# Latent attention in a two-layer decoder: keys' high and low parts in one moving operand, second-block values as whole float32, and a finer step list

## The chip, the cores and the metric

The kernel runs on one core of a Trainium2 chip. TensorE (PE) does matmuls and transposes into PSUM banks of 128 x 512 float32; VectorE (DVE), ScalarE (ACT) and GpSimd (POOL) work on SBUF and PSUM; SyncE (SP) issues the loads of weights. Each engine takes its instructions in order and waits on semaphores for the others. The metric is the device time of one execution in microseconds (us); lower is better.

## The reference

Two layers over 256 tokens of width 1024. Layer 0 mixes tokens by "forgetting" attention, layer 1 by latent attention (MLA) with 16 heads; each layer has two half-step feed-forward blocks, a layer norm after every part, and a gated input embedding. Only the latent attention is touched here:

```
c_q = rms_norm(x @ w_dq, q_norm)
q = einsum('bsc,chd->bshd', c_q, w_uq)            # 128 plain + 64 rotary columns a head
scores = (q_nope . k_nope + rope(q_rope) . k_rope) * 192**-0.5
w = softmax(where(key <= query, scores, -inf))    # two blocks of 128 queries
o = w @ v                                         # 16 heads of 128 columns
mix = o.reshape(256, 2048) @ w_o
```

The keys, the rotary key and the values come from one compressed tensor of 256 columns. All of it is float32.

## The kernel before, in words

**Float32 by parts.** A matmul of float32 values is done as three matmuls on `fp32r` operands: every operand is kept as a high part (a rounding copy, made by ScalarE) and a low part (value less high part, made by VectorE), and the product is high x high + high x low + low x high. `mm3` issues the three; `parts` makes both parts of a tile. Transposes use plain float32.

**Weights.** `Stream` loads weight blocks in the order of use into three `raw` buffers and splits each into slots (`hl`, and tiles lent by others: `ota`, `otb`, `qk`, `fs`). A split is one ScalarE copy and one VectorE subtraction, 512 to 1024 columns wide. When a split is made depends on a running estimate of each engine's time (`S.busy`) in `pump`, or on steps in the list: `f n` splits until n units are ready, `a` starts a split's copy when its load should have landed, `l` issues the subtraction left open by `a`.

**The step list.** The latent attention (`mla`) is a list of steps, `ORDER`, played one by one; each step issues instructions to one or more engines, and the list alone sets in which order each engine meets them. The steps of head h:
- `gen h`: 15 matmuls into one bank of ring `h` give the head's keys (right half) and queries (left half), then parts into `qk[h % 2]`.
- `QK h`: scores into a bank of ring `tr`. Query block 0 needs keys 0 to 127 (columns 0 to 127 of the bank), block 1 all 256 keys (columns 128 to 383). Each block gets the three products of `mm3` and two for the rotary part (`zT` with the high and the low part of `kr`).
- `sm h`: VectorE adds the mask and takes the row's minimum of the negated score (two instructions, L1470), ScalarE exponentiates and sums (L1475).
- `div h how`: a reciprocal and two scalings, on VectorE (0) or ScalarE (1).
- `T h`: three transposes of 128 columns (block 0; block 1 with keys 0 to 127; block 1 with keys 128 to 255), then parts into `PT`, of which there is one buffer.
- `AV h`: values times weights into a bank of ring `h`: three 256-wide matmuls with the values of keys 0 to 127, three 128-wide ones with those of keys 128 to 255; then parts into `otb` or `ota`.
- `O h t`: the head's share of the output product, six 512-wide matmuls for one half of the tokens.

`V g t` makes the values of four heads for keys 128t to 128t+127, `vlo` their low part. `rope`, `rot`, `zT`, `zs`, `zU` and `rc` prepare rotary queries. Rings `h` and `tr` have two banks each, `y` four.

Of the kernel before, what the change touches and what calls it, by code (L numbers as in the profile page):

```python
# [46 lines left out]
ORDER = (  # L47
# [26 lines left out]
)  # L74


# [14 lines left out]
class Recorder:  # L91
# [7 lines left out]
    def pump(self, *a, **k):  # L99
        pass  # L100

    lend = reclaim = check = load = busy = pair = split = split_pieces = ahead = later = split_now = fill = pump
    between, hl, hold = {}, {}, False


class Stream:
# [173 lines left out]
    def pair(self, n):  # L280

        self.busy(act=n)
        self.dve_t = max(self.dve_t, self.act_t + 100)
        self.busy(dve=n)

# [112 lines left out]
class Trunk:  # L398
# [97 lines left out]

    def parts(self, hi, lo, src):

        self.nc.scalar.activation(hi, src, AF.Copy)  # L499
        self.nc.vector.tensor_tensor(lo, src, hi.bitcast(F32), op=ALU.subtract)  # L500
        self.S.pair(cols(src))

    def transposed(self, t, src, halves=(0, 1), ring="tr"):

# [767 lines left out]
    def mla(self, li):  # L1272
# [34 lines left out]
        def V(g, t):  # L1307
            w = self.use(("kvv", g))
            ps = vps[g, t] = self.bank(("h", "y", "tr")[VRING[g][t]])
            for k in range(2):  # L1310
                self.mm3(
                    ps, lambda i: self.ckv[:, i, 256 * k + 128 * t : 256 * k + 128 * t + 128],
                    lambda i: w[:, i, 512 * k : 512 * k + 512], k == 0, k == 1,
                )
            o = v[t, g] = self.tl([128, 2, 512], F32R, "g4", 5)
            nc.scalar.activation(o[:, 0, :], ps, AF.Copy)
            S.busy(act=512)

        def vlo(g, t):
# [107 lines left out]
        st, PT = {}, {}  # L1427

        def gen(h):
            if h == 0:  # L1430
                home["qk"] = self.own([128, 2, 2, 512], F32R, "qk")
            ps = self.bank("h")
            hp, s = h // 2, h % 2
            w = self.use(("kvk", hp))
            for k in range(2):
                self.mm3(
                    ps[:, 256:512], lambda i: w[:, i, 256 * k + 128 * s : 256 * k + 128 * s + 128],
                    lambda i: self.ckv[:, i, 256 * k : 256 * k + 256], k == 0, k == 1,
                )
# [7 lines left out]
            self.parts(o[:, 0, :], o[:, 1, :], ps)  # L1447
# [15 lines left out]
        def softmax(h):  # L1463
# [3 lines left out]
            P = self.tl([128, 768], F32, "P", 2)[:, 0:384]  # L1467
            seg = ((0, 128), (128, 384))
            for q, (c0, c1) in enumerate(seg):
                nc.vector.tensor_tensor_reduce(  # L1470
                    out=b[:, c0:c1], in0=b[:, c0:c1], in1=self.mask[:, c0:c1],
                    op0=ALU.add, op1=ALU.min, scale=-scale, scalar=3.0e38, accum_out=nm[:, q : q + 1],
                )
            for q, (c0, c1) in enumerate(seg):
                nc.scalar.activation(  # L1475
                    P[:, c0:c1], b[:, c0:c1], AF.Exp, bias=nm[:, q : q + 1], scale=-1.0,
                    accum_out=su[:, q : q + 1],
                )
            self.S.busy(act=900, dve=600)
            st[h] = P, su  # L1480

        def divide(h, how):
            P, su = st[h]
            nc.vector.reciprocal(su[:, 0:2], su[:, 0:2])
            for q, (c0, c1) in enumerate(((0, 128), (128, 384))):
                if how == 0:
                    nc.vector.tensor_scalar(P[:, c0:c1], P[:, c0:c1], su[:, q : q + 1], None, op0=ALU.mult)
# [8 lines left out]
        def T(h):  # L1496
# [6 lines left out]
            PT[h] = o  # L1503

        OT = []

# [5 lines left out]
        def AV(h):  # L1512
            if h in (0, 10):
                OT.append(self.own([128, 4, 2, 256], F32R, "ota" if h else "otb"))
            o = PT.pop(h)
# [11 lines left out]
            self.parts(ot[:, 0, :], ot[:, 1, :], ps[:, 0:256])  # L1527

        y = [[None] * 2 for _ in range(2)]

# [15 lines left out]
        def hold(x):  # L1546
# [1 line left out]

        steps = dict(
            dq=dq, rms=rms, dqs=dq_scale, cqT=cq_transpose, V=V, vlo=vlo, qr=q_rope, rope=rope, rc=rope_copy, rot=rotate, zT=zT_first,  # L1550
            zs=z_split, zU=zT_last, gen=gen, QK=QK, sm=softmax, div=divide, T=T, AV=AV, O=O, y=room, hold=hold,
            f=S.fill, a=S.ahead, l=S.later, XT=lambda t, n: self.XT(t, (n,)),
            exp=lambda: self.ready_for(AF.Exp), gb=lambda: self.load_gb(li, 1),
            lend=lambda: S.lend("qk"), ln=lambda t: self.ln(t, y[t], ALPHA, LN_EPS),
# [119 lines left out]
```

## Time and profile before

| | |
|---|---|
| time, median of 3 runs (range) | 1069.97 us (1069.09 to 1071.38) |
| the profiled execution: time, span | 1069.07 us, 1067.3 us |
| mean granted TensorE clock | 0.998 |
| PE records | 7236 |
| latent attention, some 705 to 835 us of the span | 130 us |

The time of a run includes some 1.8 us around the span. In rows of groups the numbers after the bar are busy time in us and the mean of one instruction in ns, then the idle time of the engine just before them. PE matmuls are pipelined, so what one costs is read from the start of one to the start of the next. A plain float32 matmul appears as two records, one on `fp32r` or a transpose as one.

### The profile page before, as it was taken

What the parts mean: (1) busy time and instruction counts of PE and PEld (TensorE: products, weight loads), DVE (VectorE), ACT (ScalarE), POOL (GpSimd) and SP (SyncE); (2) the same over time, 40 slices, a digit from 0 to 9 for tenths busy, and PEclk for the clock granted to TensorE, in tenths of its full rate; (3) what the DMA queues carried; (4) which work ended last, traced back from release to release, by engine and by line L of the source; (5) the groups of instructions that cost most, each with busy time, mean ns of one, the idle gap of its engine ahead of it and who ended that gap; (6) DMA issues with size and microseconds to landing.
All of it is one profiled execution on the core that took longest, in us unless ns stands there. A gap on an engine that the chain in (4) does not pass through costs nothing.

```text
span 1067.3 us, 17503 instructions
## 1 busy us (share of the span) xinstructions
PE 1056.7 (99%) x7236; PEld 970.6 (91%) x7236; DVE 718.1 (67%) x1029; ACT 542.6 (51%) x805; POOL 68.1 (6%) x94
## 2 busy tenths in 40 slices
PE   9999999999999999999999999999999999999996
PEld 8989998999889999998899998989999889898986
DVE  6675555878797545458966464578887886454566
ACT  5564442667645434444565454436675466354431
POOL 0000000233200000000330000000000000000000
PEclk9999999999999999999999999999999999999999
DMA  8885643543348655454487555413434568555502
GB/s 299 325 295 215 247 162 119 186 175 121 115 180 301 232 186 192 146 203 139 169 294 259 180 194 187 154 59 123 137 140 158 198 244 308 181 204 182 191 4 79
DMA packets 33091, 199.58 MB, mean 187 GB/s; under 512 B 3698, under 2 KB 5490, under 8 KB 12148
## 3 DMA queue, kind: packets, MB, share of 16 engines
q1 hardware_dynamic: 33012, 198.47, 51.8%
q8 instruction: 57, 0.93, 0.4%
q14 instruction: 22, 0.18, 0.1%
HBM read 197.40 MB, written 1.05 MB: 186 GB/s over the span
## 4 chain that ended last, share of the span: by engine, by line
PE 97%; issue 1%; POOL 0%; DVE 0%; ACT 0%; DMA 0%; SPq 0%; DVEq 0%; ACTq 0%; POOLq 0%
PE y L490 36%; PE h L490 35%; PE tr L490 23%; PE tr L494 2%; DMA raw<-in_w_dram 0%; PE h L494 0%; PE tr L1087 0%; DVE x L575 0%; POOL fs L957 0%; POOL fs L950 0%; ACT hl L194 0%; SPq L360 0%; SPq L476 0%; POOL fs L956 0%; ACT hl L232 0%
## 5 line engine op out<-in xcount | busy, mean ns | idle before, releaser
L195 DVE TENSOR_TENSOR hl<-raw,hl 128x1024 fp32r<-128x1024 f32 (+2 forms) x260 | 305.7, 1194 | 146.7 <-ACT hl L194 146.1
L194 ACT ACTIVATE hl<-raw 128x1024 fp32r<-128x1024 f32 (+2 forms) x260 | 262.9, 1031 | 183.4 <-PE y L490 97.5
L490 PE MATMUL h<-xT,hl 128*128 128x256 f32 x1584 | 187.8, 278 | 1.1 <-DVE hl L234 0.5
L490 PEld LDWEIGHTS h<-xT,hl 128*128 128x128 f32 x1584 | 184.3, 189 | 2.5 <-ACT xT L499 0.9
L490 PE MATMUL y<-hl,g 128*128 128x512 f32 x792 | 185.6, 390 | 0.0
L490 PEld LDWEIGHTS y<-hl,g 128*128 128x128 f32 x792 | 147.5, 188 | 29.8
L490 PE MATMUL tr<-xT,hl 128*128 128x256 f32 x1464 | 170.8, 277 | 0.0
L490 PEld LDWEIGHTS tr<-xT,hl 128*128 128x128 f32 x1464 | 168.6, 188 | 0.5
L490 PE MATMUL h<-hl,xT 128*128 128x512 f32 (+2 forms) x294 | 65.2, 373 | 0.0
L490 PEld LDWEIGHTS h<-hl,xT 128*128 128x128 f32 x294 | 51.9, 188 | 9.7 <-DVE xT L500 0.3
L490 PE MATMUL y<-hl,xT 128*128 128x512 f32 (+3 forms) x330 | 59.7, 331 | 0.0
L490 PEld LDWEIGHTS y<-hl,xT 128*128 128x128 f32 x330 | 50.1, 188 | 5.6 <-ACT xT L499 0.4
L567 POOL TENSOR_TENSOR rs<-ve,mhalf 128x1 f32<-128x1 f32 x16 | 15.1, 943 | 619.3 <-DVE ve L566 619.3
L500 DVE TENSOR_TENSOR g<-P,g 128x512 fp32r<-128x512 f32 x38 | 26.3, 693 | 26.6 <-ACT g L499 26.6
L490 PE MATMUL y<-hl,otb 128*128 128x512 f32 x168 | 42.9, 396 | 0.0
L499 ACT ACTIVATE xT<-tr 128x512 fp32r<-128x512 f32 x28 | 16.2, 597 | 48.8 <-PE tr L494 48.8
L499 ACT ACTIVATE g<-P 128x512 fp32r<-128x512 f32 x38 | 24.0, 632 | 32.7 <-DVE P L684 32.7
L195 DVE TENSOR_TENSOR qk<-raw,qk 128x1024 fp32r<-128x1024 f32 (+2 forms) x23 | 28.0, 1217 | 16.1 <-ACT qk L194 16.1
L195 DVE TENSOR_TENSOR otb<-raw,otb 128x1024 fp32r<-128x1024 f32 (+1 forms) x22 | 26.5, 1206 | 17.7 <-ACT otb L194 17.7
L490 PEld LDWEIGHTS y<-hl,otb 128*128 128x128 f32 x168 | 30.2, 188 | 5.6
L194 ACT ACTIVATE otb<-raw 128x1024 fp32r<-128x1024 f32 (+1 forms) x22 | 22.9, 1039 | 19.4 <-PE y L490 10.8
L194 ACT ACTIVATE qk<-raw 128x1024 fp32r<-128x1024 f32 (+2 forms) x23 | 24.0, 1045 | 16.3 <-PE tr L490 6.6
(264 smaller groups left out, 1431.9 us busy)
## 6 DMA issues: line engine op xcount, KB each, us to landing
raw<-in_ffn_in_dram SPq DMA_DIRECT2D x85, 1024.0 KB, 5.0
raw<-in_ffn_out_dram SPq DMA_DIRECT2D x44, 1024.0 KB, 5.0
raw<-in_pg_dram SPq DMA_DIRECT2D x8, 1024.0 KB, 4.8
raw<-in_mo_dram SPq DMA_DIRECT2D x8, 1024.0 KB, 4.7
raw<-in_kq_dram SPq DMA_DIRECT2D x8, 640.0 KB, 4.1
gb<-in_ln_g_dram SPq DMA_DIRECT2D x8, 512.0 KB, 5.8
gb<-in_ln_b_dram SPq DMA_DIRECT2D x8, 512.0 KB, 7.7
raw<-in_fk_dram SPq DMA_DIRECT2D x4, 1024.0 KB, 4.8
```

The source lines that it names most:

```text
L194: nc.scalar.activation(hi, src, AF.Copy)
L195: nc.vector.tensor_tensor(lo, src, hi.bitcast(F32), op=ALU.subtract)
L490: self.nc.tensor.matmul(out, lhsT, rhs, start=start, stop=stop)
L494: self.nc.tensor.transpose(out, in_, self.ident)
L499: self.nc.scalar.activation(hi, src, AF.Copy)
L500: self.nc.vector.tensor_tensor(lo, src, hi.bitcast(F32), op=ALU.subtract)
L567: nc.gpsimd.tensor_tensor(rs, ve, self.mhalf, op=ALU.pow)
```

## The change

**Scores.** For query block 0 the high query part meets the key's high and low part side by side, as one 256-wide moving operand (`o[:, :, 256:384]`), and the rotary queries meet the high and low rotary keys likewise (`kr[:, 0 : r + 1 : r, 0:128]`). The bank then holds two partial sums for block 0, in columns 0 to 127 and 128 to 255; the low query part (128 wide) goes to the first. Block 1 moves to columns 256 to 511 and keeps its five matmuls.

**Softmax.** `sm` is divided into `mi` and `ex`. `mi` has a new first instruction: VectorE adds the mask to the second partial sum and writes it to SBUF; that tile takes the mask's place in the first masking instruction. The reciprocal is a step of its own, `rec`. Five divisions (heads 2, 3, 4, 10 and 12) go to ScalarE.

**Values.** Those of keys 128 to 255 (`V g 1`) stay whole float32, with no low part and no `vlo`. The third transposed block is copied whole by ScalarE (`tr`, into the tile `negc`, one buffer), and parts are made of the other two only. `AV` ends in one plain float32 matmul of 128 columns.

**Steps.** The making of parts is taken out of `gen`, `T` and `AV` into steps: `ga`, `ta`, `oa` for the high and `gd`, `td`, `od` for the low parts. The list is a new one.

```diff
-            for q0, c0, c1 in ((0, 0, 128), (128, 128, 384)):
-                w = c1 - c0
-                self.mm3(
-                    b[:, c0:c1], lambda i: o[:, i, q0 : q0 + 128],
-                    lambda i: o[:, i, 256 : 256 + w], True, False,
-                )
-                for i in (0, 1 + (h % 2 if h < 8 else 1)):
-                    self.mm(b[:, c0:c1], zT[:, h, q0 : q0 + 128], kr[:, i, 0:w], False, i > 0)
+            r = 1 + (h % 2 if h < 8 else 1)
+            two = b[:, 0:256].rearrange("p (i c) -> p i c", i=2)
+            self.mm(two, o[:, 0, 0:128], o[:, :, 256:384], True, False)
+            self.mm(b[:, 0:128], o[:, 1, 0:128], o[:, 0, 256:384], False, False)
+            self.mm(two, zT[:, h, 0:128], kr[:, 0 : r + 1 : r, 0:128], False, True)
+            self.mm3(
+                b[:, 256:512], lambda i: o[:, i, 128:256], lambda i: o[:, i, 256:512], True, False)
+            for i in (0, r):
+                self.mm(b[:, 256:512], zT[:, h, 128:256], kr[:, i, :], False, i > 0)
...
+            t = P[:, 384:512]
+            nc.vector.tensor_tensor(t, b[:, 128:256], self.mask[:, 0:128], op=ALU.add)
+            seg = ((0, b[:, 0:128], t), (128, b[:, 256:512], self.mask[:, 128:384]))
...
-            self.parts(o[:, 0, :], o[:, 1, :], b[:, 0:384])
+            raw = self.tl([128, 384], F32, "negc", 1)[:, 0:128]
+            left["T", h] = o[:, 0, 0:256], o[:, 1, 0:256], b[:, 0:256]
+            left["raw", h] = raw, b[:, 256:384]
...
-            for m, (i, jj) in enumerate(((0, 0), (0, 1), (1, 0))):
-                self.mm(
-                    ps[:, 128:256], v[1, g][:, i, c : c + 128], o[:, jj, 256:384], False, m == 2
-                )
+            self.mm(ps[:, 128:256], v[1, g][:, c : c + 128], raw, False, True)
+            S.busy(pe=128)
...
-    "f 3", "div 1 0", "rc 0", "f 2", "vlo 1 1", "V 2 0", "f 2", "gen 2", "T 0", "f 2", "gen 3", "f 1", "AV 0",
+    "f 2", "gen 3", "f 2", "tr 0", "ga 3", "AV 0", "rc 1", "y", "oa 0", "T 1", "gd 3", "l", "ta 1", "td 1", "a",
```

Where instructions stand. First TensorE, from the transposes of head 1 (`tr<-ident,P`) over the scores of head 2 (`tr<-qk`, `tr<-fs,xT`) to the value product of head 1 (`h<-PT,g4`), before:

```order
L494 MATMUL tr_7395<-ident_68,P_7311 128x128 x3
L490 MATMUL tr_7408<-qk_7221 128x128 x3
L490 MATMUL tr_7408<-fs_6382,xT_72 128x128 x2
L490 MATMUL tr_7408<-qk_7221 128x256 x3
L490 MATMUL tr_7408<-fs_6382,xT_72 128x256 x2
L490 MATMUL y_7421<-hl3_7267,otb_7381 128x512 x3
L490 MATMUL y_7422<-hl3_7267,otb_7381 128x512 x3
L490 MATMUL h_7441<-PT_7399,g4_7071 128x256 x3
L490 MATMUL h_7441<-PT_7399,g4_7046 128x128 x3
```

and now, where `negc` is the raw block:

```order
L510 MATMUL tr_7391<-ident_68,P_7307 128x128 x3
L506 MATMUL tr_7412<-qk_7220 128x256
L506 MATMUL tr_7412<-qk_7220 128x128
L506 MATMUL tr_7412<-fs_6382,xT_72 128x256
L506 MATMUL tr_7412<-qk_7220 128x256 x3
L506 MATMUL tr_7412<-fs_6382,xT_72 128x256 x2
L506 MATMUL h_7429<-PT_7395,g4_7071 128x256 x3
L506 MATMUL h_7429<-negc_7396,g4_7046 128x128
L506 MATMUL y_7388<-hl3_7276,otb_7379 128x512 x3
L506 MATMUL y_7389<-hl3_7276,otb_7379 128x512 x3
```

Ten score matmuls have become eight and six value matmuls four, and head 0's output product now stands behind head 1's value product.

ScalarE at the same place, from the keys of head 3 (`qk`) to the copy of head 1's transposes, before; `ota<-y` is a rotary copy, `hl<-raw` a split's copy:

```order
L499 ACTIVATE qk_7221<-h_7363 128x512
L499 ACTIVATE otb_7381<-h_7382 128x256
L1375 ACTIVATE ota_7157<-y_7270 128x8x64
L202 ACTIVATE hl8_7393<-raw_7107 128x512
L499 ACTIVATE PT_7399<-tr_7395 128x384
L194 ACTIVATE hl9_7403<-raw_7107 128x768
```

and now:

```order
L519 ACTIVATE qk_7220<-h_7361 128x512
L1402 ACTIVATE ota_7156<-y_7266 128x8x64
L519 ACTIVATE otb_7379<-h_7380 128x256
L519 ACTIVATE PT_7395<-tr_7391 128x256
L215 ACTIVATE hl8_7400<-raw_7106 128x512
L519 ACTIVATE negc_7396<-tr_7391 128x128
L207 ACTIVATE hl9_7405<-raw_7106 128x768
```

The copy of the first two transposed blocks has come ahead of the split's copy, and the raw block's copy stands behind it.

VectorE around the masking of head 4, before, from the low part of a weight to the divisions:

```order
L195 TENSOR_TENSOR hl7_7534<-raw_7361,hl7_7534 128x768
L500 TENSOR_TENSOR qk_7221<-h_7541,qk_7221 128x512
L500 TENSOR_TENSOR PT_7563<-tr_7559,PT_7563 128x384
L1470 ISA tr_7566,nm_7577<-tr_7566,mask_69 128x128
L1470 ISA nm_7577 128x1
L1470 ISA tr_7566,nm_7577<-tr_7566,mask_69 128x256
L1470 ISA nm_7577 128x1
L206 TENSOR_TENSOR hl1_7539<-raw_7406,hl1_7539 128x1024
L1484 RECIPROCAL su_7578<-su_7578 128x2
L1487 TENSOR_SCALAR P_7579<-P_7579,su_7578 128x128
L1487 TENSOR_SCALAR P_7579<-P_7579,su_7578 128x256
```

and now:

```order
L208 TENSOR_TENSOR hl7_7528<-raw_7359,hl7_7528 128x768
L523 TENSOR_TENSOR qk_7220<-h_7533,qk_7220 128x512
L523 TENSOR_TENSOR PT_7555<-tr_7551,PT_7555 128x256
L1511 TENSOR_TENSOR P_7579<-tr_7568,mask_69 128x128
L1514 ISA tr_7568,nm_7577<-tr_7568,P_7579 128x128
L1514 ISA nm_7577 128x1
L1514 ISA tr_7568,nm_7577<-tr_7568,mask_69 128x256
L1514 ISA nm_7577 128x1
L219 TENSOR_TENSOR hl1_7559<-raw_7408,hl1_7559 128x1024
L1533 RECIPROCAL su_7578<-su_7578 128x2
```

The add has come in ahead of the masking, the low part of the transposes is narrower, and the two divisions have gone to ScalarE.

More of the change, by code (lines that the diff above doesn't have):

```diff
@@ L100, in pump @@
         pass
-    lend = reclaim = check = load = busy = pair = split = split_pieces = ahead = later = split_now = fill = pump
+    lend = reclaim = check = load = busy = pair = follow = split = split_pieces = ahead = later = split_now = fill = pump
     between, hl, hold = {}, {}, False
@@ L282, in pair, with follow @@
         self.busy(act=n)
+        self.follow(n)
+    def follow(self, n):
         self.dve_t = max(self.dve_t, self.act_t + 100)
@@ L497, in parts, with high, low @@
     def parts(self, hi, lo, src):
+        self.high(hi, src)
+        self.low(hi, lo, src)
+    def high(self, hi, src):
         self.nc.scalar.activation(hi, src, AF.Copy)
+        self.S.busy(act=cols(src))
+    def low(self, hi, lo, src):
         self.nc.vector.tensor_tensor(lo, src, hi.bitcast(F32), op=ALU.subtract)
-        self.S.pair(cols(src))
+        self.S.follow(cols(src))
     def transposed(self, t, src, halves=(0, 1), ring="tr"):
@@ L1314, in V @@
                 )
-            o = v[t, g] = self.tl([128, 2, 512], F32R, "g4", 5)
-            nc.scalar.activation(o[:, 0, :], ps, AF.Copy)
+            if t:
+                o = v[t, g] = self.tl([128, 512], F32, "g4", 5)
+                nc.scalar.activation(o, vps.pop((g, t)), AF.Copy)
+            else:
+                o = v[t, g] = self.tl([128, 2, 512], F32R, "g4", 5)
+                nc.scalar.activation(o[:, 0, :], ps, AF.Copy)
             S.busy(act=512)
@@ L1425, in zT_last, with high, g, low @@
             S.busy(act=512)
-        st, PT = {}, {}
+        st, PT, left = {}, {}, {}
+        def high(f):
+            def g(h):
+                hi, _, src = left[f, h]
+                self.high(hi, src)
+            return g
+        def low(f):
+            return lambda h: self.low(*left.pop((f, h)))
+        def raw_copy(h):
+            self.high(*left.pop(("raw", h)))
         def gen(h):
@@ L1446, in gen @@
             o = home["qk"][:, h % 2]
-            self.parts(o[:, 0, :], o[:, 1, :], ps)
+            left["gen", h] = o[:, 0, :], o[:, 1, :], ps
         def QK(h):
@@ L1466, in softmax, with exps, recip @@
             su = self.tl([128, 4], F32, "su", 2)
-            P = self.tl([128, 768], F32, "P", 2)[:, 0:384]
-            seg = ((0, 128), (128, 384))
-            for q, (c0, c1) in enumerate(seg):
+            P = self.tl([128, 768], F32, "P", 2)
+            t = P[:, 384:512]
+            nc.vector.tensor_tensor(t, b[:, 128:256], self.mask[:, 0:128], op=ALU.add)
+            seg = ((0, b[:, 0:128], t), (128, b[:, 256:512], self.mask[:, 128:384]))
+            for q, (c0, src, more) in enumerate(seg):
                 nc.vector.tensor_tensor_reduce(
-                    out=b[:, c0:c1], in0=b[:, c0:c1], in1=self.mask[:, c0:c1],
+                    out=src, in0=src, in1=more,
                     op0=ALU.add, op1=ALU.min, scale=-scale, scalar=3.0e38, accum_out=nm[:, q : q + 1],
                 )
-            for q, (c0, c1) in enumerate(seg):
+            S.busy(dve=900)
+            st[h] = P, su, nm, seg
+        def exps(h):
+            P, su, nm, seg = st[h]
+            for q, (c0, src, _) in enumerate(seg):
                 nc.scalar.activation(
-                    P[:, c0:c1], b[:, c0:c1], AF.Exp, bias=nm[:, q : q + 1], scale=-1.0,
+                    P[:, c0 : c0 + cols(src)], src, AF.Exp, bias=nm[:, q : q + 1], scale=-1.0,
                     accum_out=su[:, q : q + 1],
                 )
-            self.S.busy(act=900, dve=600)
+            S.busy(act=900)
             st[h] = P, su
+        def recip(h):
+            P, su = st[h]
+            nc.vector.reciprocal(su[:, 0:2], su[:, 0:2])
         def divide(h, how):
             P, su = st[h]
-            nc.vector.reciprocal(su[:, 0:2], su[:, 0:2])
             for q, (c0, c1) in enumerate(((0, 128), (128, 384))):
@@ L1501, in T @@
             o = self.tl([128, 2, 384], F32R, "PT", 1)
-            self.parts(o[:, 0, :], o[:, 1, :], b[:, 0:384])
-            PT[h] = o
+            raw = self.tl([128, 384], F32, "negc", 1)[:, 0:128]
+            left["T", h] = o[:, 0, 0:256], o[:, 1, 0:256], b[:, 0:256]
+            left["raw", h] = raw, b[:, 256:384]
+            PT[h] = o, raw
         OT = []
@@ L1514, in AV @@
                 OT.append(self.own([128, 4, 2, 256], F32R, "ota" if h else "otb"))
-            o = PT.pop(h)
+            o, raw = PT.pop(h)
             ps = self.bank("h")
@@ L1521, in AV @@
                 )
-            for m, (i, jj) in enumerate(((0, 0), (0, 1), (1, 0))):
-                self.mm(
-                    ps[:, 128:256], v[1, g][:, i, c : c + 128], o[:, jj, 256:384], False, m == 2
-                )
+            self.mm(ps[:, 128:256], v[1, g][:, c : c + 128], raw, False, True)
+            S.busy(pe=128)
             ot = ot_of(h)
-            self.parts(ot[:, 0, :], ot[:, 1, :], ps[:, 0:256])
+            left["AV", h] = ot[:, 0, :], ot[:, 1, :], ps[:, 0:256]
         y = [[None] * 2 for _ in range(2)]
@@ L1550, in mla @@
             dq=dq, rms=rms, dqs=dq_scale, cqT=cq_transpose, V=V, vlo=vlo, qr=q_rope, rope=rope, rc=rope_copy, rot=rotate, zT=zT_first,
-            zs=z_split, zU=zT_last, gen=gen, QK=QK, sm=softmax, div=divide, T=T, AV=AV, O=O, y=room, hold=hold,
+            zs=z_split, zU=zT_last, gen=gen, QK=QK, mi=minima, ex=exps, rec=recip, div=divide, T=T, AV=AV,
+            ga=high("gen"), gd=low("gen"), ta=high("T"), tr=raw_copy, td=low("T"), oa=high("AV"), od=low("AV"), O=O, y=room, hold=hold,
             f=S.fill, a=S.ahead, l=S.later, XT=lambda t, n: self.XT(t, (n,)),
```

2 lines of the change are left out of this document (1 added, 1 removed), and 59 rows, old and new, of the table ORDER.

## The prediction

> **What bounds the kernel now.** I read the page first: its busy shares and its chain of waits.
>
> ```profile
> span 1067.3 us, 17503 instructions
> PE 1056.7 (99%) x7236; PEld 970.6 (91%) x7236; DVE 718.1 (67%) x1029; ACT 542.6 (51%) x805; POOL 68.1 (6%) x94
> PE 97%; issue 1%; POOL 0%; DVE 0%; ACT 0%; DMA 0%; SPq 0%; DVEq 0%; ACTq 0%; POOLq 0%
> ```
>
> TensorE is busy for 99% of the span and carries 97% of the chain, so a matmul that goes away shortens the kernel, unless a wait takes its place. The change touches only the latent attention, so next come the sums of that stretch (columns after the length: PE, PEld, DVE, ACT, POOL busy, granted clock, DMA share, GB/s).
>
> ```profile
> 702.00:838.00 136.00, 135.92 (x897) 123.70 (x896) 113.89 (x252) 84.39 (x184) 2.09 (x3) 1.00 0.39 137
> ```
>
> PE is full here too, at full clock. VectorE stands at 113.9 of 136 us (84%), ScalarE at 62%. So this stage is bound by how many matmuls PE issues, and VectorE is the engine with little room. Third, TensorE's order of time, where the start of one group less the start of the one before is what that group cost.
>
> ```profile
> 745.83 0.80 PE L490 MATMUL h<-PT,g 128*128 128x256 f32 x6
> 746.47 0.50 PE L490 MATMUL tr<-qk 128*128 128x128 f32 x3
> 746.80 0.39 PE L490 MATMUL tr<-fs,xT 128*128 128x128 f32 x2
> 747.03 0.57 PE L490 MATMUL tr<-qk 128*128 128x256 f32 x3
> 747.44 0.40 PE L490 MATMUL tr<-fs,xT 128*128 128x256 f32 x2
> 747.67 0.85 PE L490 MATMUL h<-fs,hl 128*128 128x256 f32 x6
> 748.36 1.18 PE L490 MATMUL h<-gb,hl 128*128 128x256 f32 x9
> ```
>
> This is one head: the value product (six matmuls, three 256 and three 128 wide), the scores (ten, five of each width), and keys and queries. The three 128-wide score matmuls took 746.80 - 746.47 = 0.33 us, 0.11 each; the six 256-wide ones from 747.67 took 0.69, 0.115 each. A 128-wide matmul with fp32r operands costs as much as one twice as wide. That is what the change turns on. Last, three rows of the chain, for steady prices.
>
> ```profile
> 17.47 10.88 PE tr L490 x96
> 311.01 0.87 PE tr L494 x8
> 743.44 1.15 PE tr L490 x10
> ```
>
> A 256-wide matmul in a long run is 10.88/96 = 0.113 us, a transpose (128 wide, plain float32) 0.87/8 = 0.109, a head's ten score matmuls 1.15 by the chain and 747.67 - 746.47 = 1.20 by the starts.
>
> **Scores.** Five 128-wide matmuls become two 256-wide and one 128-wide; the second query block keeps its five. Eight remain: 7 x 0.115 + 0.11 = 0.92 us. Saved per head: 0.23 (from 1.15) to 0.28 (from 1.20); I take 0.25.
>
> By the Trainium skill ("TensorE: Matmul & The Clock Gate", section "Wait — 56ns, not 53.3ns?") a warm matmul takes its columns at 2.4 GHz plus about 2.5 ns, an estimate of 56 ns for 128 columns and 109 for 256. By it the scores would be 0.83 us before and 0.82 after, and nothing would be saved; the rows above (0.33 us for three) disagree, and the measurement decides. What that rule would do as a mechanism is a rival below.
>
> **Second values.** Three 128-wide fp32r matmuls become one on plain float32. The only plain float32 product in the trace is the warm-up at the start, 384 wide, one instruction and two records:
>
> ```profile
> 1.21 1.65 PE L466 MATMUL y<-mask 128*128 128x384 f32 x2 [1.21 <-POOL mhalf L450]
> 2.65 1.06 PE L494 MATMUL tr<-ident 128*128 128x128 f32 x4
> L466 PE MATMUL y<-mask x2: 847/927/1007, 1.2 to 2.0; 128*128 128x384 f32 x2
> ```
>
> The second record starts at 2.0 and the next work at 2.65: 0.65 us for 384 columns, 0.22 for 128. The transposes right behind it, at the same early pace, take at most 1.06/4 = 0.27, later ones 0.109. So a record of 128 columns goes at about a transpose's pace, and the new product costs 2 x 0.109 = 0.22 us. Its upper end takes the first record's 0.80 us (1.2 to 2.0): 0.80/0.65 of that, 0.27. Its lower end is one matmul's 0.11, if the second record were hidden. The head's value product was 746.47 - 745.83 = 0.64; after it is 3 x 0.115 + 0.22 = 0.57. I take a saving of 0.09, between that 0.07 and the 0.11 that steady 0.11 us rows would give (0.33 against 0.22).
>
> Together 0.34 us a head, 5.4 us over 16 heads. The ends: (0.23 + 0.02) x 16 = 4.0 with the dearer product, (0.28 + 0.22) x 16 = 8.0 with its second record hidden.
>
> **What the other engines gain and lose.**
>
> ```profile
> L500 DVE TENSOR_TENSOR PT<-tr,PT 128x384 fp32r<-128x384 f32 x16 | 8.8, 549 | 0.7 <-ACT PT L499 0.7
> L1487 DVE TENSOR_SCALAR P<-P,su 128x256 f32<-128x256 f32 x16 | 5.6, 348 | 0.0
> L1470 DVE CUSTOM_DVE_ANT_0 tr<-tr,mask 128x128 f32<-128x128 f32 x16 | 4.7, 292 | 0.0
> L1487 DVE TENSOR_SCALAR P<-P,su 128x128 f32<-128x128 f32 x16 | 4.6, 287 | 0.6
> L500 DVE TENSOR_TENSOR otb<-h,otb 128x256 fp32r<-128x256 f32 x10 | 4.2, 416 | 0.5 <-ACT otb L499 0.5
> L1321 DVE TENSOR_TENSOR g<-y,g 128x512 fp32r<-128x512 f32 x3 | 2.0, 682 | 0.0
> L499 ACT ACTIVATE qk<-h 128x512 fp32r<-128x512 f32 x16 | 9.6, 599 | 9.8 <-PE h L490 9.8
> L499 ACT ACTIVATE PT<-tr 128x384 fp32r<-128x384 f32 x16 | 7.9, 492 | 2.3 <-PE tr L494 2.3
> L499 ACT ACTIVATE otb<-h 128x256 fp32r<-128x256 f32 x10 | 3.8, 383 | 0.1
> ```
>
> VectorE loses four low parts of values (4 x 0.68), a third of each transposed low part (16 x (0.55 - 0.42) = 2.1) and five divisions that move to ScalarE (5 x 0.64 = 3.2); it gains 16 adds of the second score half. An add of 128 columns is 0.42 less a further 0.13, so 0.29, as the 128-wide masking row: +4.6. Net -3.4 us. ScalarE gains a separate copy of the raw block (0.38 + 0.27 against 0.49, +0.16 x 16 = 2.6) and the five divisions (about 0.65 each, +3.3): 90 us. All of that lies beside PE, so I cost it at nothing; where the cover fails it returns as a wait, next. SyncE's loads and GpSimd's steps stand in the same order in both programs; the DMA share of 0.39 leaves room for weights wanted 4% sooner.
>
> **The new order's waits.** The trace shows nearly none now, and the list replaces them all, so I count the matmul time that covers each chain. Between the transposes of head 1 and its value product the old list has scores and an output product (1.20 + 1.37 us); the new one has the scores alone, 0.92 us.
>
> ```profile
> 742.55 0.60 ACT L499 ACTIVATE qk<-h 128x512 fp32r<-128x512 f32 x1 [0.17 <-PE h L490]
> 742.92 0.52 PE L494 MATMUL tr<-ident,P 128*128 128x128 f32 x3
> 743.12 0.38 ACT L499 ACTIVATE otb<-h 128x256 fp32r<-128x256 f32 x1
> 743.41 0.59 ACT L1375 ACTIVATE ota<-y 128x512 f32<-128x512 f32 x1
> 743.88 0.63 ACT L202 ACTIVATE hl<-raw 128x512 fp32r<-128x512 f32 x1
> 744.40 0.49 ACT L499 ACTIVATE PT<-tr 128x384 fp32r<-128x384 f32 x1
> ```
>
> Here the transposes end near 743.25, so that product could start at 743.25 + 0.92 = 744.17 and end 0.57 later, at 744.74. ScalarE's new order there is keys, rotary copy, head 0's value copy, the 256-wide copy, a weight piece, the raw copy: from 742.55 that gives 0.60, 0.59, 0.38, 0.38 to 744.50, then 0.63 and 0.27 to 745.40. The float32 product needs the raw copy and ends at 745.62: 0.88 us of wait, with the weight piece (0.63) standing in front of the raw copy and the second copy's VectorE part (0.42, to 744.92) hidden under it. Behind the waiting product stand head 0's output and head 4's keys, all of PE. The second place is head 4, between scores and transposes:
>
> ```profile
> 757.62 0.40 PE L490 MATMUL tr<-fs,xT 128*128 128x256 f32 x2
> 759.82 0.29 DVE L1470 CUSTOM_DVE_ANT_0 tr<-tr,mask 128x128 f32<-128x128 f32 x1
> 761.89 0.55 DVE L1487 TENSOR_SCALAR P<-P,su 128x128 f32<-128x128 f32 x2
> 763.09 0.49 PE L494 MATMUL tr<-ident,P 128*128 128x128 f32 x3
> ```
>
> The last two score matmuls begin at 757.62 and take 0.23, so masking starts 2.0 us after their end, behind other VectorE work; the division ends at 762.44, 0.65 before the transposes. The new list moves two output products (six 512-wide matmuls, 1.37 us) from after these scores to before them. The cover falls from 5.2 to some 3.7 us; VectorE's queue ahead of the masking is as long as before, so masking starts about 0.7 us after the scores, plus 0.29 for the add and 2.62 (759.82 to 762.44) to the divided rows: 3.6, and ScalarE's division adds a change of engine. I count 0.15. The other short covers (values of heads 11, 13, 15) stay as they were, with shorter copies; 0.1 for all. Sum of new waits 1.1 us; ends 0 (a wait in one place lets both engines run ahead for the next) and 3 (eight such places at 0.3 to 0.4).
>
> **Sum.** -5.4 + 1.1 = -4.3 us. The profiled execution took 1069.07 us (span 1067.3 and 1.8 around it), which gives 1064.8; the median of the runs is 1069.97, 0.9 higher, which gives 1065.7. I say 1065.2.
>
> **Rivals.** (1) The waits eat the gain: 3 us of them or more, 1067.2 to 1069.5. For it: VectorE at 85% of the shortened stage (110.5 of 130.6). Against: the trace shows PE full under a list with the same VectorE load.
> (2) Slower: the score-to-transpose chain of every head paces PE, since the add lengthens it by 0.29 at the head of the queue and the scores no longer cover 0.25 of it. It decides from 0.34 us of wait a head, where 5.4 us are gone; at 0.5 a head the time is 1069.97 - 5.4 + 8 = 1072.6. Against it: 0.65 us to spare at head 4, and covers above 4 us for nearly all other heads.
> (3) A narrow matmul costs its columns: 128 wide at half of 0.115, 0.058. Then the scores go from 5 x 0.058 + 5 x 0.115 = 0.865 to 0.863 and the values lose 0.22 - 0.17 = 0.05: +0.7 over 16 heads, +1.1 of waits, 1071.8, slower. Against it speak the 1.20 us for ten, so the chance is small. The Trainium skill ("TensorE: Matmul & The Clock Gate", the section named above) states it as a rule.
> (4) The second record of the float32 product hides and no wait appears: -6.5 or more, below 1063.2.
>
> **Chances.** My forecast, 1063.2 to 1067.2: 0.66. Rival (1) 0.16, half of it still over 0.2% faster. Rival (2) 0.07, (3) 0.04, (4) 0.07. Differences under 0.2% (2.1 us) can hardly be told from none here, so faster means below 1067.8: 0.66 + 0.07 + 0.08 = 0.81; slower 0.08, with some of (2) and (3) ending inside the bound; same 0.11. The range for 8 in 10 leaves out the slower cases, the far end of (1) and part of (4): 1063.0 to 1068.5.
>
> **What would show it.** In the profile after: 48 records fewer on PE (7188; 32 from the scores, 16 net from the values); a head's eight score matmuls within 0.95 us and the float32 product near 0.22; the latent stage about 4 us shorter, every other stage unchanged; a wait of near 0.9 us before or within head 1's value product, ended by ScalarE's raw copy. I am wrong if 128-wide matmuls turn out cheap where they stand alone, if the float32 record costs over 0.2 us, or if gaps open before the transposes of many heads, ended by the division.

## The result, and the profile after

The changed kernel took 1066.38 us (median of 6 runs, 1065.15 to 1068.29), the kernel before 1070.10 us (6 runs, 1069.09 to 1071.80) beside it. The ratio is 0.9968, with a 95% interval from 0.9957 to 0.9979: 3.7 us, or 0.3%, faster.

The page of the changed kernel, its head, its busy shares and its chain of waits:

```profile
span 1066.5 us, 17452 instructions
PE 1055.5 (99%) x7188; PEld 968.3 (91%) x7188; DVE 716.6 (67%) x1031; ACT 547.1 (51%) x831; POOL 66.0 (6%) x94
PE 96%; ACT 1%; DVE 1%; issue 1%; POOL 0%; DMA 0%; SPq 0%; DVEq 0%; ACTq 0%; POOLq 0%
```

There are 48 PE records fewer, and ScalarE and VectorE have come into the chain with 1% each, where TensorE alone stood. The span hides most of the gain: this execution (1068.29 us) is the slowest of the six, and ran some 2.4 us behind the profile of before by 63 us, long before the change. So what follows compares one stretch, from the first matmul of the latent attention to the first of the next feed-forward block; it is longer than the 130 us of the table ahead, which leaves out its last output products. TensorE's order of time, before (columns: start, length of the group, instruction, count):

```profile
706.37 0.51 PE L490 MATMUL y<-hl,xT 128*128 128x384 f32 x2
...
846.63 1.54 PE L490 MATMUL h<-hl,xT 128*128 128x512 f32 x6
```

and after:

```profile
708.94 0.51 PE L506 MATMUL y<-hl,xT 128*128 128x384 f32 x2
...
845.87 1.54 PE L506 MATMUL h<-hl,xT 128*128 128x512 f32 x6
```

The stage fell from 140.26 to 136.93 us, by 3.33. What follows it takes 220.65 us in both (span less end of the stage). The engine sums of the stage, with the columns of the prediction's row, before and after:

```profile
706.37:846.63 140.26, 140.18 (x915) 127.24 (x914) 117.57 (x259) 83.43 (x183) 3.01 (x4) 1.00 0.41 146
```

```profile
708.94:845.87 136.93, 136.02 (x868) 122.39 (x866) 115.50 (x261) 87.92 (x210) 3.01 (x4) 1.00 0.43 150
```

TensorE is still full at full clock. VectorE's share is 84% in both, since the stage shrank with its work (117.6 to 115.5 us); ScalarE's has gone from 59% to 64% (the prediction's 62% is of 702 to 838 us).

**What the matmuls gave.** One head's scores, and a value product with the keys' first six matmuls behind it, before:

```profile
756.62 0.53 PE L490 MATMUL tr<-qk 128*128 128x128 f32 x3
756.99 0.39 PE L490 MATMUL tr<-fs,xT 128*128 128x128 f32 x2
757.21 0.56 PE L490 MATMUL tr<-qk 128*128 128x256 f32 x3
757.62 0.40 PE L490 MATMUL tr<-fs,xT 128*128 128x256 f32 x2
757.85 2.95 PE L490 MATMUL y<-hl,otb 128*128 128x512 f32 x12
760.63 0.80 PE L490 MATMUL h<-PT,g 128*128 128x256 f32 x6
761.27 0.92 PE L490 MATMUL h<-fs,hl 128*128 128x256 f32 x6
762.03 1.23 PE L490 MATMUL h<-gb,hl 128*128 128x256 f32 x9
```

and after:

```profile
760.80 0.33 PE L506 MATMUL tr<-qk 128*128 128x256 f32 x2
760.97 0.34 PE L506 MATMUL tr<-fs,xT 128*128 128x256 f32 x1
761.15 0.52 PE L506 MATMUL tr<-qk 128*128 128x256 f32 x3
761.50 0.40 PE L506 MATMUL tr<-fs,xT 128*128 128x256 f32 x2
761.73 1.55 PE L506 MATMUL y<-hl,otb 128*128 128x512 f32 x6
763.12 0.52 PE L506 MATMUL h<-PT,g 128*128 128x256 f32 x3
763.48 0.38 PE L506 MATMUL h<-negc,g 128*128 128x128 f32 x2
763.62 0.95 PE L506 MATMUL h<-fs,hl 128*128 128x256 f32 x6
764.40 1.23 PE L506 MATMUL h<-gb,hl 128*128 128x256 f32 x9
```

Scores: 757.85 - 756.62 = 1.23 us before, 761.73 - 760.80 = 0.93 after (1.02 where transposes stand just ahead, as they do for half the heads). The median over the heads went from 1.23 to 1.02, and the sum over the 16 heads fell by 3.4 us. Values: the product itself takes 0.64 before and 0.50 after, but the two records of the float32 product end in 0.14 us and the next group then takes 0.78 instead of 0.76; with that follower, 762.03 - 760.63 = 1.40 became 764.40 - 763.12 = 1.28. Over the heads whose product has such a group of keys behind it, the median so counted fell by 0.11 (1.395 to 1.284), 1.8 us for 16 heads. Together 3.4 + 1.8 = 5.2 us; the stage fell by 3.33, so 1.9 us came back.

**What came back.** The largest wait stands before head 0's value product. TensorE, VectorE and ScalarE there:

```profile
743.45 1.22 PE L506 MATMUL h<-gb,hl 128*128 128x256 f32 x9
...
744.56 0.68 DVE L523 TENSOR_TENSOR qk<-h,qk 128x512 fp32r<-128x512 f32 x1
...
744.96 0.33 ACT L519 ACTIVATE negc<-tr 128x128 f32<-128x128 f32 x1
...
745.38 0.60 PE L506 MATMUL h<-PT,g 128*128 128x256 f32 x3 [0.70 <-ACT negc L519]
```

By the starts it costs 0.87 us (1.93 from the keys' group to the product, of which nine matmuls of 0.118 take 1.06). The profile names ScalarE's raw copy, but the first matmuls of the product do not read `negc`. They write to a bank of ring `h`, whose last reader is VectorE's low part of head 2's keys, over at 745.24, 0.15 us before the product starts. Two of the runs below settle which it was. The other waits: 0.27 us within head 1's value product, 0.35 in head 10's, 0.39 at head 12's transposes, which wait for ScalarE's division. The four make 1.88 us. Before had one such wait, of 0.31, which is gone (a further one of 0.20 both kernels have, at the keys' projection). That leaves 0.3 us in smaller pieces, which are not traced here.

### The profile page after: what moved, and what is told of

Read it like the earlier page. It is cut to its first block, busy times and chain, and to the rows that moved or that the text cites. A ratio compares the mean times of both kernels' runs of the same rounds, so it can differ in the third digit from the quotient of the medians.

```text
span 1066.5 us, 17452 instructions
## 1 busy us (share of the span) xinstructions
PE 1055.5 (99%) x7188; PEld 968.3 (91%) x7188; DVE 716.6 (67%) x1031; ACT 547.1 (51%) x831; POOL 66.0 (6%) x94
## 4 chain that ended last, share of the span: by engine, by line
PE 96%; ACT 1%; DVE 1%; issue 1%; POOL 0%; DMA 0%; SPq 0%; DVEq 0%; ACTq 0%; POOLq 0%
PE y L506 36%; PE h L506 35%; PE tr L506 23%; PE tr L510 2%; DMA raw<-in_w_dram 0%; PE h L510 0%; PE tr L1110 0%; ACT hl L207 0%; DVE x L598 0%; POOL fs L980 0%; POOL fs L973 0%; ACT P L1524 0%; DVE qk L523 0%; DVE tr L1514 0%; ACT qk L519 0%
## 5 line engine op out<-in xcount | busy, mean ns | idle before, releaser
L208 DVE TENSOR_TENSOR hl<-raw,hl 128x1024 fp32r<-128x1024 f32 (+3 forms) x260 | 306.3, 1196 | 144.5 <-ACT hl L207 143.9
L207 ACT ACTIVATE hl<-raw 128x1024 fp32r<-128x1024 f32 (+3 forms) x260 | 263.0, 1032 | 180.1 <-PE y L506 98.9
```

## The experiments

All times below are of the latent stage as cut above, from one profile each, with the ratio to the kernel before where several runs were made; the runs without one were made once. Each sum of waits is read from TensorE's starts. How far the stage's time repeats was not measured; what follows the stage, the same in all these kernels, took 220.4 to 220.7 us, so a few tenths are not read as an effect.

### Mathematics and list, apart

First the new matmuls under the list of before, each finer step right behind the step that it was taken from:

```diff
-    "f 3", "div 1 0", "rc 0", "f 2", "vlo 1 1", "V 2 0", "f 2", "gen 2", "T 0", "f 2", "gen 3", "f 1", "AV 0",
+    "gen 2", "ga 2", "gd 2", "T 0", "ta 0", "td 0", "tr 0", "f 2", "gen 3", "ga 3", "gd 3", "f 1", "AV 0",
```

> The changed matmuls under the old list: each old step is replaced by its finer steps in place, so no step moves. Latent stage means from the first 384-wide matmul to the first 512-wide one of the next feed-forward block: 140.26 us before, 136.93 after. Theory A (the matmuls carry the gain, 5.0 us, and a list only adds waits): 135.3 to 137.0 us, about 1065 to 1067 in all. Theory B (the gain needs the new list, the old one would wait in most heads): 138 us or more, over 1068.

Measured: 142.50 us, ratio 1.0018 (1.0006 to 1.0030). Theory A (135.3 to 137.0) falls: with 48 records fewer it is slower than before, and 7.4 us of waits stand against the 5.2 us saved. Then the new list with the matmuls of before (`vlo g 1` put behind `V g 1`):

```diff
-            self.mm(two, o[:, 0, 0:128], o[:, :, 256:384], True, False)
...
+                self.mm3(
+                    b[:, c0:c1], lambda i: o[:, i, q0 : q0 + 128],
+                    lambda i: o[:, i, 256 : 256 + w], True, False,
+                )
...
-            self.mm(ps[:, 128:256], v[1, g][:, c : c + 128], raw, False, True)
+            for m, (i, jj) in enumerate(((0, 0), (0, 1), (1, 0))):
```

> The old scores and the old split values under the new list (the low parts of the second values are made right behind their matmuls). Theory A: no matmul saved and the new list's waits of 1 to 2 us, so a stage of 141 to 142.5 us and about 1071 in all. Theory B: the list is worth something by itself, 139.5 us or less.

Measured: 141.01 us, ratio 1.0004 (0.9995 to 1.0013), as theory A had it. So neither half gains: 140.26 before, 141.01 with the list alone, 142.50 with the mathematics alone under this placing, 136.93 with both. Next, one part of the mathematics at a time under the new list: the scores with the values of before, and the values with the scores of before (the halves of the diff above).

> The new scores with the old split values, under the new list. Theory A with the prices as the trace after shows them: the values' 0.06 us a head is lost, so 136.9 + 1.0 = 137.9 us, between 137.4 and 138.4. With the values at the predicted 0.09: 138.4.

> The old scores with the whole float32 values, under the new list. Theory A: the scores' 0.21 us a head is lost, so 136.9 + 3.4 = 140.3 us, between 139.8 and 140.8.

Measured: scores alone 139.59 us (ratio 0.9989, 0.9978 to 1.0000), values alone 138.84 us (0.9995, 0.9986 to 1.0005). Both expectations missed, in opposite directions. From 141.01, the scores gave 1.42 us of the 3.4 that their matmuls save, and the values 2.17, more than their 1.8; the medians of the whole runs, 1.2 and 0.7 us lower than with the list alone, fit the first and leave the second open. Scores bring an add to VectorE ahead of every masking; values take low parts away from it. VectorE is busy for 120.0 us of the stage with the scores alone and for 111.5 with the values alone, which fits, though no run takes the add away by itself.

The same two parts under the list of before:

> The list of before (the finer steps directly behind the step they came from), scores as before, second values whole. Stage (first matmul of the keys' projection to the first of the next feed-forward block) was 140.26 us before, 142.50 with both edits under this list. Theory A: the add that the new scores put ahead of each masking on VectorE is what makes the new matmuls wait under the old list; then the values alone gain at least what their matmuls save and what VectorE is relieved of: 138.0 to 139.5 us. Theory B: the separate raw copy on ScalarE, next to the two-block copy, is what makes them wait: 141.0 to 142.5.

> The list of before, new scores (with the add on VectorE), second values as before. Theory A: the add alone does it, and VectorE has no relief from the values here: the stage is 141.5 to 143.5 us, with 5 us or more of new waits, most of them ended by VectorE. Theory B: no raw copy, no wait: 137.0 to 138.5 us.

Measured: values alone 140.91 us (ratio 1.0006, 0.9994 to 1.0019), scores alone 142.77 (1.0027, 1.0014 to 1.0039). The scores came out as theory A had it: 3.4 us saved and 2.5 lost make some 6 us of new waits, in fourteen places of 0.19 us or more, most of them ended by VectorE. The largest group of these in its view of waits (total us, how often, longest) is value products that wait for the low part of their transposes:

```profile
PEld h L504 <- DVE PT L521: 2.3, 5, 0.8
```

The values alone missed theory A by 1.4 us, and theory B by 0.1: without any add on VectorE, they still lost 0.65. Their two large waits (0.80 and 0.53 us) led to the next part.

### The raw copy and the other reader of its bank

This run tells the finer steps from the places of the others. It keeps the new list's matmuls, splits and divisions, and puts each finer step behind its parent, the raw copy last:

```diff
-    "f 2", "gen 3", "f 2", "tr 0", "ga 3", "AV 0", "rc 1", "y", "oa 0", "T 1", "gd 3", "l", "ta 1", "td 1", "a",
+    "tr 0", "f 2", "gen 3", "ga 3", "gd 3", "f 2", "AV 0", "oa 0", "od 0", "rc 1", "y", "T 1", "ta 1", "td 1",
```

> Both edits, the new list's positions of the matmul steps, splits and divisions, but every finer step put directly behind the step it came from (keys' parts behind the keys, transposes' parts and raw copy behind the transposes, value parts behind the value product). Theory C: the new places of the matmul steps and splits carry the list's 5.6 us (142.50 against 136.93): 136.5 to 138.0 us. Theory D: the finer steps carry it: 140 to 143 us.

Measured: 143.20 us, ratio 1.0021 (1.0010 to 1.0032). Without its finer steps the new list is 6.3 us slower, though TensorE's order is the same in both: 0.2 above the range of theory D, and far from theory C's. The groups of instructions show one reason (after the bar: busy time and mean ns; after the second: idle time of ScalarE just before them, and what ended it). The raw copies in this run, in the first run of this section, and in the changed kernel:

```profile
L519 ACT ACTIVATE negc<-tr 128x128 f32<-128x128 f32 x16 | 4.4, 278 | 15.6 <-DVE PT L523 15.6
```

```profile
L517 ACT ACTIVATE negc<-tr 128x128 f32<-128x128 f32 x16 | 4.4, 278 | 17.4 <-DVE PT L521 17.4
```

```profile
L519 ACT ACTIVATE negc<-tr 128x128 f32<-128x128 f32 x16 | 4.5, 282 | 1.4 <-DVE PT L523 1.0 <-PE tr L510 0.4
```

The raw copy reads the bank `tr`, and so does VectorE's low part. Written behind the low part, the copy waits until it has ended, about 1 us each time (17.4 and 15.6 us for 16 copies), although neither reads what the other writes. (The Trainium skill, "PSUM — Partial Sum Buffer", section "PSUM bank collisions raise a hardware error", says that two engines must be kept from one bank at the same time, reads against reads included; the waits here, 15.6 and 17.4 us, agree with a program that does so.) ScalarE's own queue then stands: weight splits, keys, value copies. In the first run that delayed, among others, the value's parts on which the output product waits:

```profile
744.17 0.28 ACT L517 ACTIVATE negc<-tr 128x128 f32<-128x128 f32 x1 [0.82 <-DVE PT L521]
...
747.64 1.20 PE L504 MATMUL y<-hl,otb 128*128 128x512 f32 x4 [0.69 <-DVE otb L521]
```

The test swaps two steps in the first run's list, for all 16 heads. Each engine then has the same instructions in the same order as there; only which of the two readers waits for the other has changed.

```diff
-    "gen 2", "ga 2", "gd 2", "T 0", "ta 0", "td 0", "tr 0", "f 2", "gen 3", "ga 3", "gd 3", "f 1", "AV 0",
+    "gen 2", "ga 2", "gd 2", "T 0", "ta 0", "tr 0", "td 0", "f 2", "gen 3", "ga 3", "gd 3", "f 1", "AV 0",
```

> Both edits under the list of before, as in the run whose latent stage took 142.50 us, but with the raw copy written ahead of the transposes' low part instead of behind it. Every engine gets the same instructions in the same order as there; what differs is which of the two readers of the transposes' bank waits for the other. In that run ScalarE stood 17.4 us in all before its 16 raw copies, each time until VectorE's low part had ended. Theory Q: that wait is a good part of the loss: ScalarE's idle time before the raw copies falls under 2 us, the product waiting for the value's low part at 747.64 starts without its 0.86 us, and the stage is 139.5 to 141.0 us. Theory A: the add on VectorE alone decides, as with the scores alone (142.77): 141.8 to 143.0 us. Theory L: the raw copy's place was the whole loss and no new list was needed: below 138.5 us.

Its raw copies:

```profile
L517 ACT ACTIVATE negc<-tr 128x128 f32<-128x128 f32 x16 | 4.6, 288 | 0.0
```

Measured: 140.25 us, ratio 0.9996 (0.9986 to 1.0006). ScalarE's 17.4 us are gone, the output product's wait fell from 0.86 to 0.23, and the stage from 142.50 to 140.25: 2.25 us for the order in which two readers of one bank are written. The whole runs agree: 1.0018 became 0.9996. Theory Q holds, and theory L falls. The rest is left: with the new matmuls under the old list's places the stage is now as long as before (140.26), so some 5.2 us of waits still eat the 5.2 us saved. The largest, about half of them, are the ones of the scores alone (0.51 us behind the keys' low part, 0.50 and 0.32 at low parts of transposes, 0.39 and 0.40 at divided rows, 0.53 at a rotary copy). The new list takes away another 3.3 us of these, and has nine of its 16 raw copies ahead of the low part. Which of its other finer steps do that, no run tells apart.

### Who holds head 0's value product

Two runs move one step each in the new list. First the raw copy goes ahead of the weight split on ScalarE:

```diff
-    "f 2", "gen 3", "f 2", "tr 0", "ga 3", "AV 0", "rc 1", "y", "oa 0", "T 1", "gd 3", "l", "ta 1", "td 1", "a",
+    "tr 0", "f 2", "gen 3", "f 2", "ga 3", "AV 0", "rc 1", "y", "oa 0", "T 1", "gd 3", "l", "ta 1", "td 1", "a",
```

> The raw copy of head 0's third transposed block goes ahead of the weight piece on ScalarE, all else as after the change. Theory R (that copy, behind the weight piece, holds head 0's value product, as the prediction had it for head 1): the wait of 0.87 us falls below 0.2 and the stage is 0.6 to 0.8 shorter than 136.93. Theory K (the product waits for its bank, whose last reader is the low part of head 2's keys on VectorE): the wait stays at 0.8 to 0.9, the stage within 0.2 of 136.93.

TensorE's order of time, at the value products of heads 0 and 1:

```profile
743.46 0.59 PE L506 MATMUL h<-PT,g 128*128 128x256 f32 x3 [0.73 <-DVE qk L523]
...
745.98 0.74 PE L506 MATMUL h<-PT,g 128*128 128x256 f32 x3 [0.44 <-DVE qk L523]
```

Measured: 137.37 us. The wait is where it was, 0.89 us by the starts, although the raw copy ended 0.43 us ahead of the product, and now the profile names VectorE's keys. The raw copy wasn't the cause, so theory R falls. The stage is 0.44 us longer, more than the 0.2 that theory K allowed: head 1's product, which had no wait in front of it, now waits 0.60 us. Second, the low part of head 2's keys goes ahead of that of head 0's transposes (and the low part of a value piece behind both):

```diff
-    "rec 1", "f 2", "div 1 0", "f 2", "gen 2", "vlo 2 0", "l", "ga 2", "f 1", "T 0", "ta 0", "td 0", "gd 2",
+    "rec 1", "f 2", "div 1 0", "f 2", "gen 2", "l", "ga 2", "f 1", "T 0", "ta 0", "gd 2", "td 0", "vlo 2 0",
```

> The low part of head 2's keys goes ahead of the low parts of head 0's transposes and of the values on VectorE. Theory K: the first matmul of head 0's value product starts some 0.6 us sooner and the rest of its wait moves to the second and to the last matmul, so the product ends 0.2 to 0.5 sooner. Theory R: no change at that product's end, within 0.1, since the raw copy stands where it stood.

```profile
743.16 0.74 PE L506 MATMUL h<-PT,g 128*128 128x256 f32 x3
...
745.82 0.74 PE L506 MATMUL h<-PT,g 128*128 128x256 f32 x3 [0.34 <-ACT hl L215]
```

Measured: 136.89 us. The wait before head 0's product fell to 0.31, and the product ends 0.36 us sooner after the keys ahead of it, so it was the keys' low part that held it (theory K). In these two runs, the changed kernel and the three with the new scores under the old list, the product starts 0.146 to 0.148 us after that low part has ended. But head 1's product now waits 0.50, again until 0.147 us after the low part of the keys that were in its bank (the profile names a weight's copy). ScalarE and VectorE are both busy for over 7 of the 8 us from 740 to 748 in the changed kernel, and here the order that served one product sooner served the next one later. The stage is the same to 0.04 us.

### What narrow matmuls and the second record cost

First the scores with the two side-by-side operands cut to 128 columns. This kernel leaves out the products with the low keys and the low rotary keys for query block 0, so its output is not the attention's:

```diff
-            self.mm(two, o[:, 0, 0:128], o[:, :, 256:384], True, False)
+            self.mm(b[:, 0:128], o[:, 0, 0:128], o[:, 0, 256:384], True, False)
...
-            self.mm(two, zT[:, h, 0:128], kr[:, 0 : r + 1 : r, 0:128], False, True)
+            self.mm(b[:, 0:128], zT[:, h, 0:128], kr[:, 0, 0:128], False, True)
```

> The two side-by-side score matmuls are cut back to 128 columns: the products of the high queries with the low keys, and of the rotary queries with the low rotary keys, are left out for query block 0 (the added tile is made from other scores, so VectorE's work is the same). Theory W (a 128-wide matmul is held by its weight load and costs what a 256-wide one does): the 15 or 16 score groups take 15.9 us as after the change, the stage within 0.3 of 136.93. Theory C (columns set the price, 0.058 a matmul): 32 x 0.058 = 1.9 us less.

```profile
759.91 0.34 PE L506 MATMUL tr<-qk 128*128 128x128 f32 x2
760.08 0.27 PE L506 MATMUL tr<-fs,xT 128*128 128x128 f32 x1
760.19 0.57 PE L506 MATMUL tr<-qk 128*128 128x256 f32 x3
760.60 0.40 PE L506 MATMUL tr<-fs,xT 128*128 128x256 f32 x2
760.83 1.56 PE L506 MATMUL y<-hl,otb 128*128 128x512 f32 x6
```

Measured: 136.72 us, 0.21 less. The eight matmuls take 760.83 - 759.91 = 0.92 us against 0.93: of 1920 columns a head 256 are gone, and 0.01 us with them. The first two take 0.17 us, whether they are 256 and 128 wide or both 128, and behind the narrow ones the three 256-wide take 0.41 instead of 0.35. So the price in theory W holds: the low keys' columns ride along free, which is what the change lives on. Its reason, the weight load, isn't tested apart from the price; the weight loads of the narrow matmuls start 0.11 us apart, which agrees with it:

```profile
760.02 0.19 PEld L506 LDWEIGHTS tr<-fs,xT 128*128 128x128 f32 x1
760.13 0.42 PEld L506 LDWEIGHTS tr<-qk 128*128 128x128 f32 x3
```

The Trainium skill ("TensorE: Matmul & The Clock Gate", section "Wait — 56ns, not 53.3ns?") would have 16 x 2 x (109 - 56) ns = 1.7 us gone here, an estimate by its figures; the 0.21 us measured disagree. That rule has no term for a weight load, and here every matmul record has one (7188 of each).

Last, the second values and the raw block in fp32r, which turns the plain float32 product into one record. The low parts of both are left out, so this output is less exact than the change's:

```diff
-                o = v[t, g] = self.tl([128, 512], F32, "g4", 5)
+                o = v[t, g] = self.tl([128, 512], F32R, "g4", 5)
...
-            raw = self.tl([128, 384], F32, "negc", 1)[:, 0:128]
+            raw = self.tl([128, 384], F32R, "negc", 1)[:, 0:128]
```

> The second values and the raw block are rounded to fp32r, so that the product of the two is one record instead of two; the low parts of both are left out of that product. Theory A (a second record costs a transpose, 0.11): 16 x 0.11 = 1.7 us less than 136.93, unless waits take it up. Rival (the second record hides, 29 ns between it and the next start): 0.5 us less at most.

```profile
754.38 0.52 PE L506 MATMUL h<-PT,g 128*128 128x256 f32 x3
754.74 0.22 PE L506 MATMUL h<-negc,g 128*128 128x128 f32 x1
754.80 0.91 PE L506 MATMUL h<-fs,hl 128*128 128x256 f32 x6
755.54 1.19 PE L506 MATMUL h<-gb,hl 128*128 128x256 f32 x9
```

Measured: 135.52 us, 1.41 less (1064.83 us in one run). With the follower counted, the value product takes 755.54 - 754.38 = 1.16 us against 1.28: the second record costs 0.12 us, near a transpose's 0.109. For 16 heads that is 1.9 us, of which 0.5 came back in waits or lies within what one profile can tell.

## Why the prediction was right, and where it was not

- **Time.** 1065.2 was said, 1066.38 measured, inside the range; the direction holds.
- **Scores.** 0.25 us a head was said, 0.21 measured. The rows it rested on, 0.11 us for a matmul of either width, hold: the narrow run bears them out, and rival (3) falls. The 0.95 us named as a sign holds for six heads; the ten others, eight of them behind transposes, take 1.01 to 1.04.
- **Values.** 0.09 was said, 0.11 measured. The float32 product does cost two records at about a transpose's pace: rival (4) falls. But they do not appear where they were looked for. The records start 0.11 and 0.03 us ahead of what follows them, and the rest stands in the next group.
- **Sum of the matmuls.** 5.2 us against 5.4.
- **Waits: the term that was too small.** 1.1 us was said, 1.9 measured, and that is most of the 1 us by which the forecast was low: 3.33 us instead of 4.3. The size of the largest agrees (0.88 said, 0.87 measured), but that is luck, since its place and cause were wrong. It stands at head 0's value product instead of head 1's (which has 0.27), and is ended by VectorE's low part of the keys, which frees the product's bank, instead of by ScalarE's raw copy. The prediction followed what the product reads and not the bank that it writes. Waits of 0.35 us at head 10 and 0.39 at head 12 (a division on ScalarE) stand against the 0.1 that it kept for the rest; head 4, where it put 0.15, has none.
- **The new list as a source of waits alone: wrong.** The working took the trace's nearly empty waits as the state that the new list spoils. The runs show that the new matmuls bring some 5.2 us of waits under the old places (7.4 with the raw copies behind the low parts), and that the list takes most of them away. The sum came out near because what was measured is the pair; that too was luck.
- **"All of that lies beside PE, so I cost it at nothing": wrong in its parts.** Under the new list the scores gave 2.0 us less than their matmuls save. VectorE's work in the stage fell by 2.1 us (3.4 was said) and ScalarE's rose by 4.5 (5.9 was said), but the add stands in every head's chain from scores to transposes.
- **Against rival (1)**, "the trace shows PE full under a list with the same VectorE load" was no argument: with the raw copy ahead under the old list VectorE is busy for 117.7 us of the stage, against 117.6 before, and 5.2 us of waits stand there. The outcome of rival (2), slower, came with the scores alone under the old list (142.77 us), but not by its chain: less than 1 us of those waits stands before the transposes of softmax weights. Under the new list one such wait is left, at head 12.
- **Overlooked:** that the separate raw copy waits for the other reader of its bank, which the section named above would have told. The new list loses only 1.0 us of ScalarE's time to it.

What two readers of one bank do to each other without that wait, no run here shows: a copy from the bank at the same time wasn't tried. Nor is it shown why the first 63 us of the changed kernel's profile went 4% slower at a full granted clock.

## What to carry to other kernels

When a change removes matmuls from a kernel whose other engines are nearly full, price the list and the matmuls as a pair: here neither was worth anything alone, in the placings tried (0.75 us lost with the list, nothing gained with the matmuls), and both together 3.3 us. For each instruction that is taken out as a step of its own, look at every other reader of the bank it reads, and write first the one whose engine comes to it first. Here that was ScalarE's copy: VectorE, with the fuller queue (84% against 59% of the stage before), came to the bank so late that the copy stood for about 1 us behind it. And when a product waits, follow the bank that it writes as well as the tiles that it reads; the name in the profile can be the other one.

## What the chip showed that was not expected

- A 128-wide fp32r matmul lets its successor start early, and the time comes back one group later: 0.17 us for the first two of a score group, 256 + 128 or 128 + 128 wide, and 0.92 or 0.93 us for the eight.
- A plain float32 product of 128 columns shows its second record as 0.03 us; the 0.12 us that it costs is only seen with the group behind it.
- The same instructions in the same order on every engine took 142.50 or 140.25 us, by which of two readers of one bank had to wait for the other.
